# Attention scores with k's low part in two zero-padded tiles instead of one shared by the two halves of a head

## The chip, the cores and the metric

One core of a Trainium2 chip runs the whole program: TensorE (PE; its weight loads are shown apart as PEld), VectorE (DVE), ScalarE (ACT), GpSimd (POOL) and the queue SP, which issues DMAs. The metric is the device time of one execution in microseconds. The kernel before takes 956.73 us, the median of three runs (956.12 to 957.03).

## The reference

Two layers of a decoder trunk over 512 tokens of width 1024, in float32. Layer 0 projects the normalised tokens once and feeds two branches, differential attention and an mLSTM; layer 1 is a gated MLP with spatial mixing. The change lies in the attention of layer 0: 8 heads, each with two score maps of 64 channels, and a causal softmax for each.

```python
s = jnp.einsum('bhcqd,bhckd->bhcqk', qi, kt).astype(jnp.float32)   # c: the two halves of a head
s = jnp.where(k_pos[None, :] <= q_pos[:, None], s, -jnp.inf)
p = jax.nn.softmax(s, axis=-1)
a = p[:, :, 0] - lam * p[:, :, 1]
return jnp.einsum('bhqk,bhkv->bhqv', a.astype(vt.dtype), vt)
```

## The kernel before, in words

Every product of float32 operands is carried by float32r passes: an operand x is split into h (its upper 12 bits) and l = x - h, and h.h + h.l + l.h is accumulated in one PSUM bank. Weights come in as `raw` by DMA from SP's queue; ACT makes `wh` (L201), DVE or POOL `wl` (L203). A projection unit (`project`, `Unit.mm`, L251) multiplies all tokens by 512 columns: 8 k-tiles, 4 output banks `pj`, 3 products each.

All engines' orders are written out by hand: the program records instructions in the order of the Python code, and a counter of k-tiles (`clock`, `tick`) says after how many of them a step of the work beside the projections is recorded (`pump`). The attention of one half (4 heads, `attention(p)`, p = 0 or 1) runs so beside the projections that follow it: at each step one row block of 128 queries of one head gets its scores (`att_a`), an earlier one its softmax difference (`att_a2`), its transposes (`att_b`, L740) and its product with v (`att_c`, L752). Within a head the row blocks go 3, 2, 1, 0, so that scores have 512, 384, 256 and 256 columns.

q and k are laid for products over 128 partitions (rows of the array). A head's 128 channels are its two halves c of 64, in partitions LO (0 to 63) and HI (64 to 127). `qa` has, for c = 0, qh in LO and ql in HI; `ka` has kh in both, so that one product gives qh.kh + ql.kh (L716). `qb` and `kb` do the same for c = 1. What is missing, qh.kl, is a second product into the same bank (L718), over the 64 partitions of that half alone: `kl` holds kl of c = 0 in LO and of c = 1 in HI.

`da_k` makes these tiles from the projection's output: ACT rounds kh into one half (L682, L683), DVE subtracts for kl (L684, L685), POOL copies kh into the other half (L686, L687). Then `da_q` makes qa and qb (L695 to L699), then the attention begins. Scores take two PSUM banks (tag "s"), one for each c; DVE adds the causal mask (L720) and takes the maximum (L721), ACT the exponential with its sum (L722).

Large tiles live in named slots (`slot`), of which a later tile takes over what an earlier one has left: A0, A1, B0, B1, M0, M1, V0, V1, W0, W1, N0, H0 to H3.

Of the kernel before, what the change touches and what calls it, by code (L numbers as in the profile page):

```python
"""Two-layer hybrid decoder trunk (differential attention + mLSTM, then gMLP) on one core.

float32 products on the tensor engine are carried by three float32r passes: every operand
x is split exactly into h (12 significant bits) and l = x - h, and h.h + h.l + l.h is
accumulated in float32.
"""
# [4 lines left out]
F32 = _my.dt.float32  # L11
# [11 lines left out]
EPS = 1e-6  # L23
# [4 lines left out]
POOL0 = (2, 5, 7, 9, 11, 13, 15)  # L28
WB = 9        # split weight tiles on chip
ATT = ((4, 4, 4, 5), (5, 5, 6, 6))  # L30
# [16 lines left out]
SOFT2 = 0  # L47
AHEAD = 7     # how far their making runs ahead of their use

# columns of l0_w_in  # L50
DA_Q, DA_K, DA_V, DA_Z = 0, 1024, 2048, 3072
ML_QK, ML_V, ML_I, ML_O, ML_Z = 4096, 5120, 6144, 6152, 7176
# rows of the table of per-channel vectors
C_DAG, C_MLG, C_CW, C_CB, C_SG, C_N = 0, 1, 3, 35, 43, 59


def hybrid_kernel(tc, x, pre_g0, w_in0, b_ig, b_fg, conv_w, conv_b, lq1, lk1, lq2, lk2,
# [8 lines left out]
    with ExitStack() as ctx:  # L66
# [13 lines left out]

# [1 line left out]
        ident = wk.tile([P, P], F32, name="ident")  # L82
# [10 lines left out]
        def rstd_of(dst, ssum, n, k):  # L93
            """dst = (ssum / n + EPS) ** -0.5"""
            nc.vector.tensor_scalar(dst, ssum, 1.0 / n, EPS, ALU.mult, ALU.add)
            nc.gpsimd.tensor_tensor(dst, dst, mhalf[:, :k], ALU.pow)

# [1 line left out]
        rows = wk.tile([P, P], F32, name="rows", tag="sz", bufs=2)  # L99
# [30 lines left out]

        # the tensor engine's clock rises while it works
        warm = wk.tile([P, 512], BF16, name="warm", tag="aT", bufs=2)
# [27 lines left out]

# [1 line left out]
        # units of 512 columns in the order in which they are computed: weights, first column,  # L162
        # k-tiles in order
        up = lambda n: list(range(n))
# [48 lines left out]
        def later(dt, fn, soft=False):  # L213
            """emit fn after dt more k-tiles' products; a soft one not while it should be quiet"""
            clock["due"].append((clock["t"] + dt, fn, soft))
# [40 lines left out]
        def project(kind, ah, al, consumer, tail=2, quiet=None):  # L256
            """quiet: the function that the consumer needs, with no other work between the outputs"""
            un = Unit(kind, ah, al)
# [25 lines left out]

        # normalised tokens, transposed and split
        def norm_transpose(i, xns, hT, lT, hf, nm):
# [11 lines left out]

# [1 line left out]
        hT = [slot(f"H{k}", f"hT{k}", F32R) for k in range(2)]  # L300
# [35 lines left out]

# [1 line left out]
        def new_mv(p):  # L338
# [73 lines left out]

        # gates of the mLSTM: log-space weights per token (columns) and per chunk (rows)
        N0 = slot("N0", "n0misc", F32, (P, 2048))
# [20 lines left out]
        def gates():  # L435
# [15 lines left out]
            for c in range(4):  # L451
                nc.tensor.matmul(gps[:, c * 8:c * 8 + 8], lhsT=grow[:, c * P:(c + 1) * P],
                                 rhs=fold, start=True, stop=True)
            # gate columns: [token, (chunk, head)]
            gview = gps[:, 0:32].rearrange("p (c g) -> p c g", c=4)
            for dst, o in ((gi, 0), (xf, 4)):
# [3 lines left out]
                                        ALU.add)  # L460
            # log_sigmoid(x) = min(x, 0) - log1p(exp(-|x|)), log1p(e) = 2 artanh(e / (2 + e))
            ee = st(16, "ee")
# [15 lines left out]
            nc.vector.scalar_tensor_tensor(lf, xf, 0.0, acc, ALU.min, ALU.subtract)  # L478
            # lambda
            ldot = st(2, "ldot")  # L480
# [7 lines left out]
            yield  # L488
            # rows: [(chunk, head), position]
            rps = pst("s", "rps")  # L490
# [14 lines left out]
            nc.vector.tensor_copy(blR, cp2[:1, 0:32])  # L505
            mrow = wk.tile([1, 32], F32, name="mrow")       # m_prev of every chunk, M at its end
            nc.vector.memset(mrow, 0.0)
# [33 lines left out]
        def pump():  # L541
            """one step of the work beside the projections; a step says how long to wait after it"""
            while bg:
                try:
                    clock["next"] = clock["t"] + (next(bg[0]) or 4)
                    break
                except StopIteration:
                    bg.pop(0)
# [43 lines left out]

# [1 line left out]
        Cst = N0[:, 0:1032].rearrange("p (h d) -> p h d", h=4)  # L594
# [59 lines left out]

# [1 line left out]
        dq, dk, dv = {}, {}, {}  # L656
# [9 lines left out]
        def da_v(p):  # L666
            dv[p] = slot(f"V{p}", f"dv{p}")
            project("nat", ah0, al0, copy_consumer(dv[p]))

        # The heads' q and k split and stacked for K = 128: with c the half of a head that the  # L670
        # partitions hold, q[c] has qh in half c and ql in the other one, k[c] has kh in both,
        # and kl[c] is in half c.
        LO, HI = slice(0, 64), slice(64, 128)

        def da_k(p, tags):
            def f(i, o):
                if i == 0:
                    if p == 1:
                        drain(ga0)
                    dk[p] = [slot(t, f"{n}{p}", F32R) for t, n in zip(tags, ("ka", "kb", "kl"))]  # L680
                ka, kb, kl = dk[p]
                nc.scalar.copy(ka[LO, i, :], o[LO, :])  # L682
                nc.scalar.copy(kb[HI, i, :], o[HI, :])  # L683
                nc.vector.tensor_tensor(kl[LO, i, :], o[LO, :], ka[LO, i, :], ALU.subtract)  # L684
                nc.vector.tensor_tensor(kl[HI, i, :], o[HI, :], kb[HI, i, :], ALU.subtract)  # L685
                nc.gpsimd.tensor_copy(ka[HI, i, :], ka[LO, i, :])  # L686
                nc.gpsimd.tensor_copy(kb[LO, i, :], kb[HI, i, :])  # L687
            project("tr", ah0, al0, f)
# [14 lines left out]
        def att_a(p, h, i):  # L703
# [8 lines left out]
            for c in range(2):  # L712
                cc = (LO, HI)[c]
                s = pst("s", f"sc{nm}{c}")
                qs = dq[p][c][:, h, i * P:(i + 1) * P]
                nc.tensor.matmul(s[:, :n2], lhsT=qs, rhs=dk[p][c][:, h, 0:n2],  # L716
                                 start=True, stop=False)
                nc.tensor.matmul(s[:, :n2], lhsT=qs[cc, :], rhs=dk[p][2][cc, h, 0:n2],  # L718
                                 start=False, stop=True)
# [6 lines left out]
        def att_a2(pr, sm, nk, r0):  # L726
            """p0 - (lam s0 / s1) p1; the output takes the 1 / s0"""
            nc.vector.reciprocal(sm[:, 2:3], sm[:, 1:2])
            nc.vector.reciprocal(r0, sm[:, 0:1])
            nc.vector.scalar_tensor_tensor(sm[:, 3:4], sm[:, 2:3], nlam, sm[:, 0:1],  # L730
                                           ALU.mult, ALU.mult)
            nc.vector.scalar_tensor_tensor(pr[:, 0, :nk], pr[:, 1, :nk], sm[:, 3:4], pr[:, 0, :nk],
                                           ALU.mult, ALU.add)
# [22 lines left out]
        def head_norm(p, h):  # L756
            """the head's rmsnorm in four steps; a mean square beyond float32 gives rstd = 0, as an
            infinite one does"""
            o = ao.pop((p, h))
# [56 lines left out]

# [1 line left out]
        yh, yl = {}, {}  # L818
# [70 lines left out]
        da_v(0)  # L889
        da_k(0, ("A0", "A1", "B1"))  # L890
        drain(gm)
# [4 lines left out]
        ml_o(0)  # L896
        da_k(1, ("M0", "M1", "B1"))
        da_q(1, ("B0", "N0"))
# [3 lines left out]
        bg.append(da_z(0, ("A0", "A1")))  # L902
        bg.append(ml_z(0, ("M0", "M1")))
        bg.append(ml_z(1, ("V0", "W0")))
        drain(ga1)
        bg.append(da_z(1, ("B0", "B1")))

# [1 line left out]
        def out_project(layer, ah, al, post_g, h1, done, y0tag):  # L909
# [41 lines left out]
        def load_h1():  # L951
            for t, n in (("W1", "h1a"), ("V1", "h1b")):
                h1t.append(slot(t, n))
# [33 lines left out]

# [1 line left out]
        ah1 = lambda k: hT1[k // 4][:, k % 4, :]  # L989
# [3 lines left out]
        for j in range(4):  # L993
            vt = slot(("A0", "A1", "M0", "M1")[j], f"v1_{j}")
            v1.append(vt)
# [43 lines left out]
        for j in range(4):  # L1039
# [6 lines left out]
            project("tr", ah1, al1, fu)  # L1046
            tg = (("B0", "B1"), ("V0", "W0"), ("N0", "A0"), ("A1", "M0"))[j]
            y1h.append(slot(tg[0], f"y1h{j}", F32R))
# [57 lines left out]
```

## Time and profile before

| | us |
|---|---|
| median of three runs | 956.73 |
| span of the profiled execution, first to last instruction | 954.5 |
| TensorE busy in it | 939.4 |
| weight loads (beside the matmuls) | 753.3 |
| DVE busy | 458.5 |
| ACT busy | 410.4 |
| POOL busy | 179.1 |

The page gives the span of the profiled execution and no time of its own around it. Ends of matmuls are modelled, and matmuls overlap; their starts are what is to be read. "issue" behind an idle time is idle that no semaphore event explains. PEclk is the granted clock of TensorE as a share of 2.4 GHz. The attention of the first half lies between some 202 and 306 us, that of the second between 327 and 432.

### The profile page before, as it was taken

What the parts mean: (1) busy time and instruction counts of PE and PEld (TensorE: products, weight loads), DVE (VectorE), ACT (ScalarE), POOL (GpSimd) and SP (SyncE); (2) the same over time, 40 slices, a digit from 0 to 9 for tenths busy, and PEclk for the clock granted to TensorE, in tenths of its full rate; (3) what the DMA queues carried; (4) which work ended last, traced back from release to release, by engine and by line L of the source; (5) the groups of instructions that cost most, each with busy time, mean ns of one, the idle gap of its engine ahead of it and who ended that gap; (6) DMA issues with size and microseconds to landing.
All of it is one profiled execution on the core that took longest, in us unless ns stands there. A gap on an engine that the chain in (4) does not pass through costs nothing.

```text
span 954.5 us, 11642 instructions
## 1 busy us (share of the span) xinstructions
PE 939.4 (98%) x4259; PEld 753.3 (79%) x4259; DVE 458.5 (48%) x955; ACT 410.4 (43%) x876; POOL 179.1 (19%) x258
## 2 busy tenths in 40 slices
PE   7999999999999999999999999999999999999997
PEld 4778888877778777778888887888888888888885
DVE  4467555656656465664443355222634343434323
ACT  5334433445566445665443335444224242433311
POOL 3210022311245214444020022000010101011000
PEclk8999999999999999999999999999999999999998
DMA  8242222312112322222343313423223232314212
GB/s 270 69 132 90 89 67 63 93 45 67 54 58 89 89 66 67 62 72 71 105 155 133 111 45 110 133 91 109 90 69 107 67 111 67 110 67 133 89 45 88
DMA packets 45039, 86.94 MB, mean 91 GB/s; under 512 B 4715, under 2 KB 5046, under 8 KB 44854
## 3 DMA queue, kind: packets, MB, share of 16 engines
q1 hardware_dynamic: 43334, 80.29, 26.5%
q0 software_dynamic: 1504, 5.78, 1.7%
q8 instruction: 33, 0.54, 0.2%
q14 instruction: 24, 0.20, 0.1%
q10 hardware_dynamic: 144, 0.13, 0.0%
HBM read 84.08 MB, written 2.11 MB: 90 GB/s over the span
## 4 chain that ended last, share of the span: by engine, by line
PE 96%; DMA 1%; DVE 1%; issue 1%; SPq 0%; ACT 0%; POOLq 0%; POOL 0%; DVEq 0%; ACTq 0%
PE pj L251 83%; PE sc L718 2%; PE ao L752 2%; PE sc L716 2%; PE vs L1058 1%; PE at L740 1%; DMA raw<-in_l_w_in_dram 1%; PE yT L823 1%; PE mN L625 1%; PE xnT L289 1%; PE mN L627 1%; PE mU L631 1%; DVE xn_b L979 1%; PE gT L445 0%; PE mS L602 0%
## 5 line engine op out<-in xcount | busy, mean ns | idle before, releaser
L203 DVE TENSOR_TENSOR wl<-raw,wh 128x512 fp32r<-128x512 f32 x250 | 172.9, 712 | 254.3 <-ACT wh L201 253.8
L201 ACT CAST wh<-raw 128x512 fp32r<-128x512 f32 x287 | 169.4, 615 | 135.9 <-PE pj L251 120.8
L251 PE MATMUL pj<-wh,hT 128*128 128x512 f32 x448 | 183.1, 409 | 0.7 <-ACT hT L292 0.7
L251 PE MATMUL pj<-hT,wh 128*128 128x512 f32 x448 | 180.8, 403 | 0.0
L251 PE MATMUL pj<-hT,wl 128*128 128x512 f32 x448 | 177.1, 395 | 0.0
L251 PE MATMUL pj<-lT,wh 128*128 128x512 f32 x448 | 177.1, 395 | 0.0
L251 PE MATMUL pj<-wh,lT 128*128 128x512 f32 x448 | 176.9, 395 | 0.0
L251 PE MATMUL pj<-wl,hT 128*128 128x512 f32 x448 | 176.6, 394 | 0.0
L251 PEld LDWEIGHTS pj<-wh,hT 128*128 128x128 f32 x448 | 85.0, 190 | 22.8 <-issue 3.4
L251 PEld LDWEIGHTS pj<-wh,lT 128*128 128x128 f32 x448 | 84.8, 189 | 19.6 <-DVE lT L293 0.6
L251 PEld LDWEIGHTS pj<-hT,wl 128*128 128x128 f32 x448 | 84.2, 188 | 20.4
L251 PEld LDWEIGHTS pj<-hT,wh 128*128 128x128 f32 x448 | 84.3, 188 | 19.6 <-issue 0.5
L251 PEld LDWEIGHTS pj<-lT,wh 128*128 128x128 f32 x448 | 84.3, 188 | 18.6
L251 PEld LDWEIGHTS pj<-wl,hT 128*128 128x128 f32 x448 | 85.1, 190 | 16.0
L203 POOL TENSOR_TENSOR wl<-raw,wh 128x512 fp32r<-128x512 f32 x38 | 52.1, 1373 | 135.5 <-ACT wh L201 131.8
L251 PE MATMUL pj<-wh,yh 128*128 128x512 f32 x128 | 51.4, 402 | 0.0
L722 ACT ACTIVATE p<-sc,nm 128x512 f32<-128x512 f32 (+3 forms) x64 | 33.7, 527 | 39.8 <-DVE nm L721 36.8
L251 PE MATMUL pj<-wh,yl 128*128 128x512 f32 x128 | 50.5, 395 | 0.0
L251 PE MATMUL pj<-wh,y1h 128*128 128x512 f32 x128 | 50.3, 393 | 0.0
L251 PE MATMUL pj<-wl,yh 128*128 128x512 f32 x128 | 50.3, 393 | 0.0
L251 PE MATMUL pj<-wh,y1l 128*128 128x512 f32 x128 | 50.3, 393 | 0.0
L1054 POOL TENSOR_TENSOR sz<-gu,sz 128x512 f32<-128x512 f32 x16 | 21.1, 1317 | 155.5 <-ACT sz L1053 155.5
(255 smaller groups left out, 1147.0 us busy)
## 6 DMA issues: line engine op xcount, KB each, us to landing
raw<-in_l_w_in_dram SPq DMA_DIRECT2D x112, 512.0 KB, 3.7
raw<-in_l_w_out_dram SPq DMA_DIRECT2D x32, 512.0 KB, 3.3
x<-in_x_dram SPq DMA_DIRECT2D x3, 512.0 KB, 9.9
nMb<-scr POOLq DMA_DIRECT2D x1, 1024.0 KB, 4.8
pg<-in_l_post_g_dram POOLq DMA_DIRECT2D x2, 512.0 KB, 4.3
h1a<-in_x_dram POOLq DMA_DIRECT2D x2, 512.0 KB, 4.2
h1b<-in_x_dram POOLq DMA_DIRECT2D x2, 512.0 KB, 4.9
out_dram<-h1a SPq DMA_DIRECT2D x4, 256.0 KB, 2.0
```

Source lines behind the costliest of these rows:

```text
L201: nc.scalar.copy(wh, raw[:, n % 2, :])
L203: eng.tensor_tensor(wl, raw[:, n % 2, :], wh, ALU.subtract)
L251: nc.tensor.matmul(self.outs[i], lhsT=a, rhs=b, start=(n == 0 and m == 0), stop=(n == len(self.ks) - 1 and m == ms[-1]))
L289: nc.tensor.transpose(b[:, k * P:(k + 1) * P], xns[:, hf, k * P:(k + 1) * P], ident)
L625: nc.tensor.matmul(o[:, 0:258], lhsT=mt[:, 0, :], rhs=va, start=True, stop=(c == 0))
L627: nc.tensor.matmul(o[:, 0:258], lhsT=mt[:, 3, :], rhs=Cst[:, h, :], start=False, stop=True)
L631: nc.tensor.matmul(u[:, 0:258], lhsT=mt[:, 4, :], rhs=va, start=True, stop=True)
L716: nc.tensor.matmul(s[:, :n2], lhsT=qs, rhs=dk[p][c][:, h, 0:n2], start=True, stop=False)
L718: nc.tensor.matmul(s[:, :n2], lhsT=qs[cc, :], rhs=dk[p][2][cc, h, 0:n2], start=False, stop=True)
L722: nc.scalar.activation(pr[:, c, :nk], s[:, :nk], AF.Exp, bias=nmx[:, c:c + 1], accum_out=sm[:, c:c + 1])
L752: nc.tensor.matmul(o[:, i * P:(i + 1) * P], lhsT=aT[:, kb * P:(kb + 1) * P], rhs=dv[p][:, kb, h * P:(h + 1) * P], start=(kb == 0), stop=(k ...
L1054: nc.gpsimd.tensor_tensor(sz, gus[i // 2][:, i % 2, :], sz, ALU.mult)
```

## The change

The tile `kl` becomes two, `kla` and `klb`. Each holds kl of its half of the heads in that half's 64 partitions, and zeros in the other 64, which POOL writes once for each p. The second score product then runs over all 128 partitions, with the same `qs` as the first; the other part of q meets the zeros. The second tile needs a slot more, so several tiles change places: the second v goes to M0, the k tiles of p = 1 to M1, A0, B1 and V1, and later tiles that stood in M0 stand in V1 (and the other way round).

```diff
-            dv[p] = slot(f"V{p}", f"dv{p}")
+            dv[p] = slot(("V0", "M0")[p], f"dv{p}")
...
-                    dk[p] = [slot(t, f"{n}{p}", F32R) for t, n in zip(tags, ("ka", "kb", "kl"))]
-                ka, kb, kl = dk[p]
+                    dk[p] = [slot(t, f"{n}{p}", F32R) for t, n in zip(tags, ("ka", "kb", "kla", "klb"))]
+                    for t, half in zip(dk[p][2:], (HI, LO)):
+                        nc.gpsimd.memset(t[half, :, :].bitcast(F32), 0.0)
+                ka, kb, kla, klb = dk[p]
...
-                nc.vector.tensor_tensor(kl[LO, i, :], o[LO, :], ka[LO, i, :], ALU.subtract)
-                nc.vector.tensor_tensor(kl[HI, i, :], o[HI, :], kb[HI, i, :], ALU.subtract)
+                nc.vector.tensor_tensor(kla[LO, i, :], o[LO, :], ka[LO, i, :], ALU.subtract)
+                nc.vector.tensor_tensor(klb[HI, i, :], o[HI, :], kb[HI, i, :], ALU.subtract)
...
-                cc = (LO, HI)[c]
...
-                nc.tensor.matmul(s[:, :n2], lhsT=qs[cc, :], rhs=dk[p][2][cc, h, 0:n2],
+                nc.tensor.matmul(s[:, :n2], lhsT=qs, rhs=dk[p][2 + c][:, h, 0:n2],
                                  start=False, stop=True)
...
-        da_k(0, ("A0", "A1", "B1"))
+        da_k(0, ("A0", "A1", "B1", "V1"))
...
-        da_k(1, ("M0", "M1", "B1"))
+        da_k(1, ("M1", "A0", "B1", "V1"))
...
-        bg.append(ml_z(0, ("M0", "M1")))
+        bg.append(ml_z(0, ("V1", "M1")))
...
-            for t, n in (("W1", "h1a"), ("V1", "h1b")):
+            for t, n in (("W1", "h1a"), ("M0", "h1b")):
...
-            vt = slot(("A0", "A1", "M0", "M1")[j], f"v1_{j}")
+            vt = slot(("A0", "A1", "V1", "M1")[j], f"v1_{j}")
...
-            tg = (("B0", "B1"), ("V0", "W0"), ("N0", "A0"), ("A1", "M0"))[j]
+            tg = (("B0", "B1"), ("V0", "W0"), ("N0", "A0"), ("A1", "V1"))[j]
```

POOL's queue before, where the k of the first half is made: the last step of the mLSTM on POOL (L612), the copies of kh into the other half, then weight splits of the unit after the next. In brackets stands what a row waits for.

```order
L612 TENSOR_TENSOR mt_1539<-mt_1539,mq 128x128 [waits Activation_49]
L686 COPY ka_1578<-ka_1578 64x512 [waits DMAHW3_49,Activation_49,Pool_49]
L687 COPY kb_1579<-kb_1579 64x512 [waits Activation_49]
L686 COPY ka_1578<-ka_1578 64x512 [waits Activation_49]
L687 COPY kb_1579<-kb_1579 64x512 [waits Activation_49]
```

The same place in the changed kernel, whose lines are numbered one or two higher:

```order
L612 TENSOR_TENSOR mt_1539<-mt_1539,mq 128x128 [waits Activation_49]
L682 MEMSET kla_1580 64x2048 [waits Pool_49]
L682 MEMSET klb_1581 64x2048
L688 COPY ka_1578<-ka_1578 64x512 [waits DMAHW3_49,Activation_49]
L689 COPY kb_1579<-kb_1579 64x512 [waits Activation_49]
L688 COPY ka_1578<-ka_1578 64x512 [waits Activation_49]
L689 COPY kb_1579<-kb_1579 64x512 [waits Activation_49]
```

Two memsets stand ahead of the copies; the same two stand at the same place of the second half. The queues of DVE, ACT and SP hold the same instructions in the same order, with the same waits.

TensorE's queue before, at the first score group of the first half, between two projection products:

```order
L251 MATMUL pj_0_1794<-wh_0_1683,lT_119 128x512
L716 MATMUL sc_1805<-ka_1578,qa_1635 128x512 [waits Activation_49,Pool_49]
L718 MATMUL sc_1805<-kl_1580,qa_1635 128x512
L716 MATMUL sc_1811<-kb_1579,qb_1636 128x512 [waits Activation_49,Pool_49]
L718 MATMUL sc_1811<-kl_1580,qb_1636 128x512
L251 MATMUL pj_0_1794<-wh_1_1699,hT_117 128x512
```

And in the changed kernel:

```order
L251 MATMUL pj_0_1797<-wh_0_1686,lT_119 128x512
L717 MATMUL sc_1808<-ka_1578,qa_1638 128x512 [waits Activation_49,Pool_49]
L719 MATMUL sc_1808<-kla_1580,qa_1638 128x512
L717 MATMUL sc_1814<-kb_1579,qb_1639 128x512 [waits Activation_49,Pool_49]
L719 MATMUL sc_1814<-klb_1581,qb_1639 128x512
L251 MATMUL pj_0_1797<-wh_1_1702,hT_117 128x512
```

No product is moved, added or taken away, and the waits are the same; the second product of each pair reads another tile (the sizes printed are those of the output).

## Rows read from the trace of the kernel before

**Rows 1.** The page, part 1: busy us (share of span) xinstructions.

```profile
PE 939.4 (98%) x4259; PEld 753.3 (79%) x4259; DVE 458.5 (48%) x955; ACT 410.4 (43%) x876; POOL 179.1 (19%) x258
```

**Rows 2.** Waits of TensorE: us in total, times, longest; first and last of four.

```profile
PE xnT L289 <- DVE xn_a L330: 3.8, 3, 3.0
...
PE pj L251 <- ACT hT L292: 0.7, 1, 0.7
```

**Rows 3.** The chain that ended last: start us, us, what; a stretch of projections alone.

```profile
65.43 48.07 PE pj L251 x207
```

**Rows 4.** Timeline: start us, us, engine, line, out<-in, size [idle before]; first score group.

```profile
202.65 0.39 PE L716 MATMUL sc<-ka,qa 128*128 128x512 f32 x1
...
202.97 0.49 PE L718 MATMUL sc<-kl,qa 64*128 64x512 f32 x1
...
203.39 0.49 PE L716 MATMUL sc<-kb,qb 128*128 128x512 f32 x1
203.81 0.18 PEld L718 LDWEIGHTS sc<-kl,qb 64*128 64x128 f32 x1 [0.24 <-issue]
203.81 0.50 PE L718 MATMUL sc<-kl,qb 64*128 64x512 f32 x1
...
204.24 0.51 PE L251 MATMUL pj<-wh,hT 128*128 128x512 f32 x1
...
204.58 0.40 PE L251 MATMUL pj<-wl,hT 128*128 128x512 f32 x1
```

**Rows 5.** Timeline: second products of the groups of 384 and of 256 columns.

```profile
208.45 0.44 PE L716 MATMUL sc<-kb,qb 128*128 128x384 f32 x1
...
208.82 0.44 PE L718 MATMUL sc<-kl,qb 64*128 64x384 f32 x1
...
213.03 0.38 PE L716 MATMUL sc<-kb,qb 128*128 128x256 f32 x1
...
213.34 0.38 PE L718 MATMUL sc<-kl,qb 64*128 64x256 f32 x1
```

**Rows 6.** Timeline: eight 16-row products of the gates (L452) and the projection behind them.

```profile
47.37 0.96 PEld L452 LDWEIGHTS gps<-fold,n0misc 16*128 16x128 f32 x8 [0.37 <-issue]
...
48.35 0.50 PE L251 MATMUL pj<-hT,wh 128*128 128x512 f32 x1
...
48.70 0.40 PE L251 MATMUL pj<-lT,wh 128*128 128x512 f32 x1
```

**Rows 7.** Timeline: eight products of 128 columns with v, and what comes next.

```profile
216.51 1.05 PE L752 MATMUL ao<-dv,aT 128*128 128x128 f32 x8
...
217.40 0.49 PE L740 MATMUL at<-ident,p 128*128 128x128 f32 x3
```

**Rows 8.** POOL: a memset, copies grouped (busy, mean ns), last copy; TensorE: the score behind.

```profile
1.31 0.20 POOL L85 MEMSET tri<- 128x128 f32 x1
...
L686 POOL CAST ka<-ka 64x512 fp32r<-64x512 f32 x8 | 6.0, 746 | 2.9 <-issue 1.9 <-ACT ka L682 0.5
...
308.90 0.96 POOL L687 CAST kb<-kb 64x512 fp32r<-64x512 f32 x1
...
327.76 0.39 PE L716 MATMUL sc<-ka,qa 128*128 128x512 f32 x1
```

**Rows 9.** Timeline: ends of two exponentials' sums, and DVE's product of p.

```profile
207.87 0.19 ACT L722 ACTIVATION_READ_ACCUMULATOR p<-sc,nm 128x1 f32 x1
...
209.66 0.75 DVE L732 SCALAR_TENSOR_TENSOR p<-p,sm 128x512 f32<-128x512 f32 x1
...
212.52 0.19 ACT L722 ACTIVATION_READ_ACCUMULATOR p<-sc,nm 128x1 f32 x1
```

**Rows 10.** All waits: DVE for the scores of TensorE, us in total, times, longest.

```profile
DVE sc L720 <- PE sc L718: 23.1, 19, 3.1
```

**Rows 11.** Windows: us, busy (x) of PE, PEld, DVE, ACT, POOL, granted clock, DMA.

```profile
10.00:20.00 10.00, 8.95 (x35) 6.22 (x36) 7.85 (x12) 5.55 (x11) 3.10 (x4) 0.78 1.02 356
...
202.00:306.00 104.00, 104.00 (x479) 80.11 (x478) 64.68 (x172) 58.20 (x158) 33.75 (x62) 1.00 0.20 61
```

## The prediction

> **What bounds the kernel now.** I read the first part of the page first: TensorE is busy 939.4 of the 954.5 us of the span, the next engine 458.5 [rows 1]. Then the waits of TensorE by releaser: there are four rows, 8.2 us in all, and the last of them is worth 0.7 us; none of the four is in the attention, they lie in the two norms, the warm-up and the first products [rows 2]. So between 202 and 432 us, where the two attention halves run between the projections' products, the end is set by how fast TensorE gets through its own queue. The view to read there is the order in time with its start times: matmuls overlap, and the distance from one start to the next is what a product costs, not its duration.
>
> A projection product (512 columns, 128 rows) costs 48.07 us / 207 = 0.232 us [rows 3]. In the first score group the same size costs more: from the 64-row product to the next 128-row one 0.42 us, from there to the next 64-row one 0.42, from there to the projection 0.43, and the second projection product still comes 0.34 after the first; the very first 64-row product comes 0.32 after the score product ahead of it [rows 4]. The weight load of a 64-row product shows 0.24 us of idle ahead of it that no event explains ("issue") [rows 4]: loads elsewhere are done under the matmul before, this one waits for it.
>
> **What the change removes.** From the first score product's start to the second projection product's start the group of 512 columns takes 204.58 - 202.65 = 1.93 us [rows 4]; five products at 0.232 are 1.16. So 0.77 us per group is lost, four times 0.19: once at each of its four boundaries between 128 and 64 rows. For the smaller shapes a boundary costs 208.82 - 208.45 = 0.37 at 384 columns and 213.34 - 213.03 = 0.31 at 256 [rows 5]; in proportion to columns a product there is worth 0.174 and 0.116, which leaves 0.196 and 0.194. The loss is the same at every size, so it belongs to the boundary and not to the columns. A second place in the program bears this out: eight 16-row products at 47.37 us have the same unexplained idle of 0.37 us ahead of their first weight load, all eight loads then run through in 0.96 us (0.12 apart at most), and the second 128-row product behind them comes 0.35 after the first [rows 6]. Few rows alone cost nothing there; going in and out does.
>
> The changed kernel has 32 score groups (2 halves, 4 heads, 4 row blocks) of four 128-row products, so all 128 boundaries go: 32 x 0.77 = 24.6 us off TensorE's queue.
>
> The bounds of that: a 256-column product has to cost 0.116 for it, and no 256-column float32r product at 128 rows on both sides stands in the trace. The nearest rows from below are the eight products of [rows 7], 217.40 - 216.51 = 0.89 us for eight, 0.111 each with a weight load for each. From above, the duration of one weight load is 0.19 us [rows 4]; if loads could not overlap each other, 256 and 384 columns would cost 0.19 and the saving falls by 16 x 4 x 0.074 + 8 x 4 x 0.016 = 5.2 us, to 19.4. I take the lower one, since loads in [rows 7] do overlap.
>
> **A rule that speaks against it.** The two 64-row products of a group start 203.81 - 202.97 = 0.84 us apart, with a full-height product between them [rows 4]; nothing of them overlaps. The Trainium skill, "TensorE: Matmul & The Clock Gate", Part 3, says that products with few rows, laid at different row groups, run at the same time, and its closing table advises slicing small contractions that way. By that rule padding throws away a chance of hiding one of the two, some 32 x 0.16 = 5 us; but that chance was not taken by the kernel before, so by the trace nothing of it is lost here.
>
> **What the change adds.** Four memsets on POOL of 64 x 2048, two ahead of each half's copies of k. The nearest rows: a memset of 128 elements per partition takes 0.20 us, a copy of 512 per partition 0.746 [rows 8]. The first scaled by 16 gives 3.2 us, the second by 4 gives 3.0; a fixed part inside these would make it less, down to some 1.6. So POOL's copies end 3 to 6.5 us later per half. Behind them in POOL's queue stand the weight splits of later units, and the score products wait for the copies. The copies end at 309.86 and the first score product that needs them starts at 327.76 [rows 8]: 17.9 us of cover, with the projection of q in between; the first half is alike. Cost nothing. Cover is gone only if one memset took over 8 us. The two subtractions on DVE stay, into two tiles instead of one. The swaps of slots (the second v into the former query slot of the mLSTM, kb of the second half into the slot of ka of the first) add no wait to any engine's row, and what the slots held is drained before. No DMA is added, and SP's queue keeps its order.
>
> **What becomes late next.** A group that TensorE reaches earlier must still find its PSUM bank free: a score bank is released by the exponential of the step before. In the first steps DVE and ACT are no faster: DVE's long product of p, which hangs on the exponentials alone, is at work from 209.66 to 210.41 [rows 9], when the second group is already computed, and only then comes DVE's next work on scores; so their times stay put. The second group's second half started at 208.45 [rows 5], and the bank's last reader ended at 207.87 + 0.19 = 208.06 [rows 9]: 0.39 us of room. TensorE would come 0.77 + 0.39 (two boundaries of its own group) = 1.16 earlier, so it waits 0.77. In the third group the room is 213.03 - (212.52 + 0.19) = 0.32 [rows 5, 9], the lead 1.16 again, the wait 0.84. Together 1.6 us. Later DVE itself waits for scores, 23.1 us over 19 of its 64 times [rows 10], so there the elementwise chain has slack to follow. I allow 1.0 us for further short waits, an estimate between 0 and 3.
>
> **The sum.** 24.6 - 1.6 - 1.0 = 22.0 us off a span of 954.5: 932.5. The page gives the span alone; the median of the timed runs, 956.7, is 2.2 above it, and I carry these 2.2 over: **934.7 us**.
>
> **The rivals.**
> - *Weight loads set the pace.* At 256 and 384 columns a product costs 0.19, the upper bound above. 19.4 saved, less 1.5 of waits: 17.9, 938.8 us. For it: no such product stands in the trace. Against: 0.111 apart in [rows 7].
> - *The elementwise chain takes over.* In 45 of 64 steps DVE does not wait for scores, and in the first steps the chain is the slower side. If that held all along, only the steps in which DVE waits would gain: 19/64 of 24.6 is 7.3, some 949 us. Against: the 23.1 us of [rows 10] are spread over both halves, and the busy shares of DVE and ACT there are 0.62 and 0.56 [rows 11].
> - *The boundary is not the cause.* If the idle came from adding a second product to a bank, or from reading q twice, the padded products would keep it, and the time would be 956.7. Against: the projections add 24 products to one bank at 0.232, the projection behind a group pays too, and so do the 16-row products of [rows 6].
> - *Slower, by the clock.* The granted clock is 1.00 (2.4 GHz) in the attention and fell to 0.78 in the 10 us of the start around and behind a wait of TensorE of 3.0 us at once [rows 2, 11]. If the new waits in the first groups brought the lower level, 1.2 GHz, it would cost half of each stretch at it; the change comes out slower once more than 44 us of the attention are run at the lower level (22 us lost), for instance 960 with 50. Against: the waits worked out are under 0.9 us each, three times shorter than that one.
>
> **How the numbers follow.** The forecast (931 to 937, that is 20 to 25 saved) gets 0.66, weight loads 0.17, the elementwise chain 0.08, no effect 0.05, slower 0.02; 0.02 is left for a larger gain, below 930. Forecast and weight loads hold 0.83; their ends, with the bounds of the waits (0 to 3 us) and of the load, are 930.5 and 941.5. That is the range. The measurement tells 0.2%, 1.9 us, from no change. Faster: 0.66 + 0.17 + 0.08 + 0.02 = 0.93; same 0.05; slower 0.02.
>
> **What would show it.** Right: in the changed kernel's order in time the four score products of 512, 384 and 256 columns start about 0.23, 0.17 and 0.12 apart, the projection product behind them follows at once, and no weight load of a score product has unexplained idle ahead of it; the stretch from the first score product to the last is about 22 us shorter, and the waits of TensorE gain a row "sc <- ACT p" of one to two us, in the second and third group. Starts 0.19 apart at 256 columns show the rival of weight loads; idle ahead of the second product of each pair, still there, shows that the boundary was not it; a row of score products that wait for POOL would show that the memsets are not covered; many rows of waits for DVE or ACT between 202 and 432 us show the elementwise chain. A granted clock under 0.95 in the attention would show the fourth.

## The result, and the profile after

The changed kernel takes 935.43 us (median of four runs, 934.87 to 935.66) against 956.42 for the kernel before beside it: a ratio of 0.9783, 95% interval 0.9769 to 0.9797, so 21.0 us or 2.2% less. The span of its profiled execution is 933.5 us.

Part 1 of its page, to be set against [rows 1]:

```profile
PE 916.7 (98%) x4259; PEld 749.0 (80%) x4259; DVE 458.0 (49%) x955; ACT 408.6 (44%) x876; POOL 185.7 (20%) x262
```

TensorE has the same 4259 matmuls and is busy 22.7 us less. DVE and ACT do the same work; POOL does 6.6 us more. The first score group in the order in time (columns as in [rows 4]):

```profile
203.37 0.39 PE L717 MATMUL sc<-ka,qa 128*128 128x512 f32 x1
203.60 0.39 PE L719 MATMUL sc<-kla,qa 128*128 128x512 f32 x1
203.83 0.40 PE L717 MATMUL sc<-kb,qb 128*128 128x512 f32 x1
204.06 0.39 PE L719 MATMUL sc<-klb,qb 128*128 128x512 f32 x1
204.29 0.39 PE L251 MATMUL pj<-wh,hT 128*128 128x512 f32 x1
204.52 0.39 PE L251 MATMUL pj<-wl,hT 128*128 128x512 f32 x1
```

All starts are 0.23 apart, and from the first to the sixth it is 1.15 us, where [rows 4] had 1.93. The fourth group, of 256 columns:

```profile
217.92 0.28 PE L719 MATMUL sc<-kla,qa 128*128 128x256 f32 x1
218.04 0.28 PE L717 MATMUL sc<-kb,qb 128*128 128x256 f32 x1
218.16 0.28 PE L719 MATMUL sc<-klb,qb 128*128 128x256 f32 x1
218.28 0.39 PE L251 MATMUL pj<-wh,hT 128*128 128x512 f32 x1
```

0.12 apart, where [rows 5] had 0.31. A group of 384 columns, behind the first of its products:

```profile
227.00 0.34 PE L719 MATMUL sc<-kla,qa 128*128 128x384 f32 x1
227.18 0.34 PE L717 MATMUL sc<-kb,qb 128*128 128x384 f32 x1
227.36 0.34 PE L719 MATMUL sc<-klb,qb 128*128 128x384 f32 x1
```

0.18 apart. (In groups that stand behind transposes, in both kernels, the first product's start is shown 0.03 us behind the last transpose, where transposes are 0.11 apart, and the next product 0.08 later than its columns ask for. The sum is the same; such groups are read from the second product on.) By the starts in the two traces, the stretch from the first score product to the last went from 225.2 to 204.4 us, 20.8 less. What lies before it and behind it differs by less than 1 us each, and by as much between the two traces of the changed kernel; so small differences are read below from the stretch of the scores.

What TensorE waits for in the attention, new against [rows 2]; three rows of its waits (us in total, times, longest), and one of its weight loads:

```profile
PE pj L251 <- ACT mz L869: 1.2, 1, 1.2
...
PE sc L717 <- ACT p L723: 0.6, 2, 0.3
PE pj L251 <- ACT mo L852: 0.2, 1, 0.2
...
PEld sc L717 <- ACT p L723: 2.1, 5, 0.6
```

The second group, in the timeline:

```profile
207.51 0.39 PE L251 MATMUL pj<-wh,lT 128*128 128x512 f32 x1
207.91 0.44 PE L717 MATMUL sc<-ka,qa 128*128 128x384 f32 x1
208.19 0.34 PE L719 MATMUL sc<-kla,qa 128*128 128x384 f32 x1
208.84 0.44 PE L717 MATMUL sc<-kb,qb 128*128 128x384 f32 x1 [0.31 <-ACT p L723]
209.12 0.34 PE L719 MATMUL sc<-klb,qb 128*128 128x384 f32 x1
209.30 0.40 PE L251 MATMUL pj<-wh,hT 128*128 128x512 f32 x1
```

From 207.51 to 209.30 it is 1.79 us; 0.23 and four times 0.174 are 0.93. So the wait costs 0.86 us: 0.17 ahead of the first score product, 0.48 ahead of the third, and 0.10 behind each of these two. The row of waits names only 0.31 of it: a matmul counts as busy until its modelled end, and part of the wait lies under that; and the loads of the two products that wait start with them, at 207.91 and 208.84, each followed by the next load only 0.11 later, so that the product behind comes late too. The third group loses as much:

```profile
212.06 0.60 PE L741 MATMUL at<-ident,p 128*128 128x128 f32 x4
212.69 0.39 PE L717 MATMUL sc<-ka,qa 128*128 128x256 f32 x1
...
213.49 0.38 PE L717 MATMUL sc<-kb,qb 128*128 128x256 f32 x1 [0.30 <-ACT p L723]
...
213.84 0.39 PE L251 MATMUL pj<-wh,hT 128*128 128x512 f32 x1
```

1.78 us against 4 x 0.11 + 4 x 0.117 = 0.91: 0.87. The largest is at the end of a projection in the second half, where a projection bank is still being read by ACT:

```profile
403.74 0.40 PE L251 MATMUL pj<-wh,lT 128*128 128x512 f32 x1
405.36 0.50 PE L251 MATMUL pj<-wh,hT 128*128 128x512 f32 x1 [1.23 <-ACT mz L869]
405.70 0.39 PE L251 MATMUL pj<-wl,hT 128*128 128x512 f32 x1
```

1.96 us for two products, 1.5 too many. With some 0.4 at the other bank (mo) and 0.3 in the second and third group of the second half the waits of the attention come to 3.9 us. Together with the 20.8 that were gained this is 24.7, which is what the boundaries were worked out to cost.

On the other side, DVE's wait for scores, which was 23.1 us in [rows 10]:

```profile
DVE sc L721 <- PE sc L719: 5.2, 7, 2.3
```

DVE used to wait for TensorE; now it does so for less than a quarter of that time.

### The profile page after: what moved, and what is told of

It is laid out like the page before. It is cut to its first block, busy times and chain, and to the rows that moved or that the text cites. A ratio compares the mean times of both kernels' runs of the same rounds, so it can differ in the third digit from the quotient of the medians.

```text
span 933.5 us, 11645 instructions
## 1 busy us (share of the span) xinstructions
PE 916.7 (98%) x4259; PEld 749.0 (80%) x4259; DVE 458.0 (49%) x955; ACT 408.6 (44%) x876; POOL 185.7 (20%) x262
## 4 chain that ended last, share of the span: by engine, by line
PE 89%; DVE 4%; ACT 4%; issue 1%; DMA 1%; POOL 1%; SPq 0%; POOLq 0%; DVEq 0%; ACTq 0%
PE pj L251 79%; PE vs L1059 2%; PE ao L753 2%; DVE nm L722 1%; ACT wh L201 1%; ACT p L723 1%; DMA x<-in_x_dram 1%; PE sc L717 1%; PE yT L824 1%; PE mN L625 1%; PE sc L719 1%; PE at L741 1%; PE xnT L289 1%; PE mU L631 1%; PE mN L627 1%
## 5 line engine op out<-in xcount | busy, mean ns | idle before, releaser
L251 PE MATMUL pj<-wh,hT 128*128 128x512 f32 x448 | 179.8, 401 | 2.0 <-ACT mz L869 1.2
L251 PE MATMUL pj<-wl,y1h 128*128 128x512 f32 x128 | 50.3, 393 | 0.0
```

The costliest lines, as they stand in the source:

```text
L251: nc.tensor.matmul(self.outs[i], lhsT=a, rhs=b, start=(n == 0 and m == 0), stop=(n == len(self.ks) - 1 and m == ms[-1]))
```

## The experiments

Each is measured against runs of the kernel before on the same chip (956.1 to 956.8 us). Times are medians.

| run | us | what is in it |
|---|---|---|
| before | 956.4 | four boundaries between 128 and 64 rows per score group |
| changed | 935.43, again 935.46 | none |
| e1_rows64 | 956.05 | the changed kernel, second products over 64 rows |
| e2_one_padded | 944.91 | two boundaries, one 64-row product |
| e3_adjacent64 | 942.01 | two boundaries, two 64-row products side by side |
| e4_memsets3 | 936.03 | three times the memsets |
| e5_no_second | 933.29 | no second products |
| e10_no_mask | 930.33 | changed, without DVE's mask |
| e9_no_second_no_mask | 924.02 | neither |
| e6, e7 (first steps) | 937.09, 937.70 | early score groups later |
| e11_shifted | 936.29 | the same, later steps kept in place |
| e12_two_on_pool | 934.63 | two weight splits from DVE to POOL |

### Was it the boundary?

**e1_rows64**: the number of rows undone, all else as changed.

```diff
-                nc.tensor.matmul(s[:, :n2], lhsT=qs, rhs=dk[p][2 + c][:, h, 0:n2],
+                cc = (LO, HI)[c]
+                nc.tensor.matmul(s[:, :n2], lhsT=qs[cc, :], rhs=dk[p][2 + c][cc, h, 0:n2],
                                  start=False, stop=True)
```

> The changed kernel with one part undone: the second score product runs over the 64 partitions of its half again, reading kla or klb there. The two tiles, their slots, the four memsets and the order of all queues stay as changed. Theory (each change between 128 and 64 rows in TensorE's queue costs about 0.19 us, 128 of them): the whole gain goes, 956.4 us give or take 1, with the starts 0.42, 0.37 and 0.31 apart as before, and the memsets and slots cost nothing. Rival (part of the gain comes from the new places of the tiles or from POOL's memsets): between 936 and 952.

956.05 us, ratio to the kernel before 0.9997 (0.9988 to 1.0007). The whole gain hangs on the rows; the slots, the second tile and the memsets cost and give nothing that can be measured.

**e2_one_padded**: only c = 0 padded.

```diff
-                nc.tensor.matmul(s[:, :n2], lhsT=qs, rhs=dk[p][2 + c][:, h, 0:n2],
+                cc = (slice(0, P), HI)[c]
+                nc.tensor.matmul(s[:, :n2], lhsT=qs[cc, :], rhs=dk[p][2 + c][cc, h, 0:n2],
                                  start=False, stop=True)
```

> As the changed kernel, but only c = 0 has the zero-padded second product; for c = 1 it runs over 64 partitions. Two boundaries between 128 and 64 rows per group instead of none, 64 in all. Theory: 64 x 0.19 = 12.3 us of the 24.6 come back, and the early waits of TensorE are shorter by about 1 us than in the changed kernel: 945 us (944 to 947). Theory that the 64-row product itself costs 0.39 more, wherever it stands: the same 945. Rival (elementwise chain sets the pace beyond the first gain): nearer 937.

944.91 us. The first group in its timeline, from its third product on:

```profile
203.91 0.40 PE L717 MATMUL sc<-kb,qb 128*128 128x512 f32 x1
204.23 0.50 PE L720 MATMUL sc<-klb,qb 64*128 64x512 f32 x1
204.66 0.50 PE L251 MATMUL pj<-wh,hT 128*128 128x512 f32 x1
205.00 0.39 PE L251 MATMUL pj<-wl,hT 128*128 128x512 f32 x1
```

0.32, 0.43 and 0.34 where 0.23 each would do: 0.40 us for two boundaries. Half the boundaries, half the loss. That does not yet tell a boundary from a product that is dear wherever it stands; the next run does.

**e3_adjacent64**: both second products over 64 rows again, but next to each other.

```diff
-            for c in range(2):
-                s = pst("s", f"sc{nm}{c}")
...
+            for c, full, first in ((0, True, True), (0, False, False), (1, False, True), (1, True, False)):
+                cc = slice(0, P) if full else (LO, HI)[c]
+                k = dk[p][c if full else 2 + c]
+                nc.tensor.matmul(ss[c][:, :n2], lhsT=qs[c][cc, :], rhs=k[cc, h, 0:n2],
+                                 start=first, stop=not first)
```

> As e1 (both second products over 64 partitions), but the four products of a group stand in the order 128 rows (c = 0), 64 rows (c = 0, partitions 0 to 63), 64 rows (c = 1, partitions 64 to 127), 128 rows (c = 1). Two boundaries per group, two 64-row products next to each other. Boundary theory: 945 us (944 to 947), and the second 64-row product starts 0.23 (512 columns) behind the first. If the change from one half of the rows to the other costs as much as one from 128 to 64: three boundaries, 950.5. Theory that each 64-row product costs 0.39: 956.4. Rule of the Trainium skill, TensorE: Matmul & The Clock Gate, Part 3 (products at different row groups run at the same time): the second starts a few ns behind the first and some 5 us more are saved, 940.

942.01 us. Its first group:

```profile
202.68 0.39 PE L719 MATMUL sc<-ka,qa 128*128 128x512 f32 x1
203.00 0.49 PE L719 MATMUL sc<-kla,qa 64*128 64x512 f32 x1
203.01 0.49 PE L719 MATMUL sc<-klb,qb 64*128 64x512 f32 x1
203.43 0.50 PE L719 MATMUL sc<-kb,qb 128*128 128x512 f32 x1
203.76 0.40 PE L251 MATMUL pj<-wh,hT 128*128 128x512 f32 x1
204.00 0.40 PE L251 MATMUL pj<-wl,hT 128*128 128x512 f32 x1
```

The two 64-row products start together and share one slot of 0.42 us (by the starts they are 0.01 us apart or less in all groups that do not wait for a bank). From the first score product to the second projection product it is 1.32 us: 1.93 before, 1.15 with padding. A 64-row product is therefore not dear in itself: here the second costs nothing. Going in and out costs 0.39, and overlapping saves one product: 0.23, 0.17 or 0.12. So a single pair is better padded at all three sizes, and by little at 512. The time lies 2 us above what the rule of overlap would have given (940), and 3 below the boundary theory alone; the stretch of the scores is 4.0 us shorter than in e2 (209.8 against 213.8), where 5 were expected. By the steps some 0.7 of the missing 1 us lies in the second and the fourteenth, where TensorE waits for a bank; in the second and third group it is the second of the two 64-row products that waits, so these pairs do not overlap.

**e4_memsets3**: POOL's cover.

```diff
-                    for t, half in zip(dk[p][2:], (HI, LO)):
+                    for t, half in 3 * tuple(zip(dk[p][2:], (HI, LO))):
```

> The changed kernel with each memset written three times, so four more of 1.8 us ahead of each half's copies on POOL, 7.2 us per half. Theory (POOL's copies have room: in the changed kernel the copies of the second half end at 304.62 and the first score product that needs them starts at 318.12, 13.5 us): the same time, 935.4 give or take 0.7. Rival (the copies are on TensorE's path): up to 2 x 7.2 us longer, 950.

936.03 us (934.79 to 936.79): no more than the scatter, and the stretch of the scores is the same 204.4 us. The last memset and the last copy of the second half, and (TensorE) the first score product that needs them:

```profile
303.94 1.80 POOL L682 MEMSET klb<- 64x2048 f32 x1
...
310.86 0.61 POOL L689 CAST kb<-kb 64x512 fp32r<-64x512 f32 x1
...
318.53 0.39 PE L717 MATMUL sc<-ka,qa 128*128 128x512 f32 x1
```

With 7.2 us more on POOL there are still 7 us of room.

### What comes next?

**e5_no_second**: the second products left out.

```diff
                 nc.tensor.matmul(s[:, :n2], lhsT=qs, rhs=dk[p][c][:, h, 0:n2],
-                                 start=True, stop=False)
-                nc.tensor.matmul(s[:, :n2], lhsT=qs, rhs=dk[p][2 + c][:, h, 0:n2],
-                                 start=False, stop=True)
+                                 start=True, stop=True)
```

> The changed kernel without any second score product (the term qh.kl is left out), 64 products fewer, no boundary added. Price of the padded products by their spacing in the changed kernel: 2 x (8 x 0.231 + 8 x 0.176 + 16 x 0.117) = 10.3 us. Theory (TensorE's queue is the bound, the elementwise chain follows but for short waits): 10.3 less some 2.5 us of more waits in the second and third group and at the two places where a projection bank is late: 927.7 us (926 to 930). Rival (after the first gain DVE and ACT set the pace): under 4 us saved, 932 to 935.

933.29 us: 2.1 us saved, not 7.7. The theory that TensorE's queue goes on being the bound fell here, and the time lies in the range of its rival. Four rows of what TensorE waits for, and DVE's wait for scores:

```profile
PE sc L717 <- ACT p L721: 2.9, 8, 0.5
PE pj L251 <- ACT mz L867: 2.0, 1, 2.0
...
PE pj L251 <- ACT dz L829: 1.1, 1, 1.1
PE pj L251 <- ACT mo L850: 1.0, 1, 1.0
```

```profile
DVE sc L719 <- PE sc L717: 2.8, 3, 2.0
```

By the starts, steps without a wait are 0.2 to 0.5 us shorter, as 64 fewer products would have it; others are up to 1.4 longer, and the two halves together gain 1.9 us. By these rows the room that DVE and ACT had, 23.1 us of waiting in [rows 10], was nearly used up by the change itself.

**e9_no_second_no_mask** and **e10_no_mask** test that by making the chain of DVE and ACT shorter.

```diff
-                nc.vector.tensor_tensor(s[:, i * P:nk], s[:, i * P:nk], tri, ALU.add)
```

> The kernel without second score products (it took 933.3 us) and also without DVE's addition of the causal mask to the scores, so neither qh.kl nor the mask is in the output: 64 additions of 0.29 us less on DVE, 18.6 us. If the chain of DVE and ACT is what kept that kernel from its 10.3 us, the chain is shorter now by about 0.6 us per step and TensorE gets most of them: 926 to 928. Rival (it was something else, a projection bank or a weight that is late whatever DVE does): 932 to 934.

> The changed kernel without DVE's addition of the causal mask alone (the mask is missing from the output). If the chain costs the changed kernel only the waits that its trace shows, 1.7 us in the second and third group and 1.4 at two projection banks, at most these go: 933 give or take 1. If the chain holds the changed kernel back more than that: under 931.

Without the mask's addition the changed kernel takes 930.33 us and the one without second products 924.02. Between these two the second products are worth 6.3 us (7.3 by the stretch of the scores, 200.9 and 193.6), with the mask 2.1. So it was the chain that held e5 back, for the larger part: the price of 10.3 is not reached here either. 924.02 is also less than the 926 to 928 that were expected. In e10 the first half's steps (first score group to sixteenth) take 68.95 us instead of 70.54, the second's 87.31 instead of 89.18: 3.5 us of the 3.9 that were read off the changed kernel as waits. 1.5 and 0.4 of it come back at the two projection banks, 1.2 of 1.7 in the first three steps, 0.3 in the second half. The other 1.6 us of its 5.1 lie outside the attention, where the two traces of the changed kernel differ by over 1 us ahead of it and as much behind it. By the time alone, under 931, e10 would speak for a chain that costs more than its waits; by the trace it does not. DVE waits for scores again in e10:

```profile
DVE nm L721 <- PE sc L719: 14.4, 11, 2.8
```

**e6_first_steps5, e7_first_steps6, e11_shifted**: the early waits, taken by recording the second and third score group of the first half later.

```diff
-                yield ATT[p][items[n][1]] if n < len(items) else 4
+                yield (5 if p == 0 and n < 2 else ATT[p][items[n][1]]) if n < len(items) else 4
```

> The changed kernel with 5 instead of 4 k-tiles of projection between the first, second and third score group of the first half. Theory (the waits of the second and third group for the exponentials, 0.86 and 0.87 us by the starts, are made by the two groups coming too early, and a k-tile is 0.70 us of work): 0.7 us of each is filled, 934.0 against 935.4. Rival (the wait only moves to the fourth group or to the next projection): 935.4.

> The same with 6 k-tiles. Theory: both waits are filled in full, 1.7 us, 933.7 against 935.4. Rival (moved, not filled): 935.4.

> The changed kernel as it is, on the same chip and beside the two before it, as their measure: 935.4 us, give or take 0.7.

> The changed kernel with one k-tile more ahead of the second and of the third score group of the first half, and one less behind its eighth and twelfth, so that later steps stand where they stood. Theory: the early waits are filled, some 1.2 us, 934.2 against 935.4 to 935.5. Rival (the chain needs the time, wherever the wait is taken): 935.4 or a little more, with new waits near the eighth and twelfth group.

(The first step had 5 k-tiles already, so that e6 adds one and e7 three; e11 adds one at each of the two steps and takes one away at each of two later ones.) 937.09, 937.70 and 936.29 us, against 935.46 for the changed kernel beside e6 and e7: all three forecasts failed. e11 came out as its rival had it, e6 and e7 slower than even their rivals (935.4). The stretch of the scores is 206.5, 205.2 and 205.4 us, against 204.4; of the 2.2 us that e7 loses only 0.8 lies in it, and where the rest comes from is not known. At the place itself the waits did fill in part: the first three steps take 14.35 us in the changed kernel and the same in e6 with one more k-tile of 0.70 in them, 14.96 in e7 with three more. (In e6 the wait of the second group stays as it was, since the step ahead of it is no longer than before; that of the third falls to 0.2, and the fourth group gets one of 0.3.) It was lost further on: in e6 the thirteenth and fourteenth step take 14.6 us together instead of 12.3 (13.2 in e7), and in both the next unit waits at its banks:

```profile
PE pj L251 <- DVE klb L687: 1.2, 1, 1.2
```

The attention is held while a projection's last products are made (`quiet`), and a step that comes one k-tile late falls into that stretch; that this is the mechanism is read from the code and was not tried by itself. In e11 the steps that were cut to three k-tiles run without a wait (3.42 us), but the fourteenth takes 8.37 instead of 7.40 and the wait for mo is 1.1 instead of 0.2: the wait moved.

**e12_two_on_pool**: instead of the timetable, the chain.

```diff
         on_pool.update((18, n) for n in PU18)
+        on_pool.update(((7, 6), (7, 7)))
```

> The changed kernel with two of DVE's weight splits (the seventh and eighth of the unit that runs when the first half's attention begins) given to POOL; the result is the same. In the changed kernel DVE takes such a split at 209.33, after 1.35 us of waiting for ACT's cast, between the exponentials of the first group and its softmax difference. Theory: without it the second group's maxima come 1.1 us sooner, and the wait of the third group, 0.87 us, goes; that of the second (0.86), which hangs on the first group's exponentials, stays: the three first steps take 13.5 instead of 14.35 us, and the kernel 934.6 against 935.4 and 935.5. Rival (another wait takes its place): 14.35 and 935.4.

934.63 us (933.03 to 935.35), and by the trace the first three steps take 13.54 us instead of 14.35; all later ones are the same to 0.01. The wait of the third group is gone, that of the second stays. The whole, 0.8 us, is what the trace gives; the timed runs of the two kernels touch, so by them alone it is not told apart. Its median is the lowest of the versions in which no product and no mask is left out.

## Why the prediction held, point by point

- **The bound.** That TensorE's own queue set the end in the attention was right for the kernel before: e1 and e2 move by the boundaries, but for the short waits. It is no longer so behind the change (e5).
- **The price of a boundary**, 0.19 us, and the sum of 24.6 us: right (20.8 gained and 3.9 of waits). It does not fall once at each boundary, though: by the starts the five distances of a group lose 0.09, 0.19, 0.19, 0.20 and 0.11. Starts after are 0.23, 0.18 and 0.12 apart, as forecast, and e2 with half the boundaries lies 11.8 us below the kernel before beside it and 9.5 above the changed one. (The last two boundaries give less than the first two, since by then the waits take a share.)
- **256 columns at 0.116**: measured 0.118 (0.114 to 0.122 where nothing waits). The rows chosen for it were misread in part: the eight rows of [rows 7] are four products in plain float32 (`att_c` makes 80, the trace has 160 records), each recorded twice, so 0.111 is the distance from one load and pass to the next and not the cost of a product; that loads can follow so closely is what the choice needed. The rival of weight loads at 0.19 fell; a load still takes 0.19 there, but under the products before it.
- **The memsets.** 1.81 us each (a group's row of the changed kernel: count | busy us, mean ns | idle before), near the lower end of 1.6 to 3.2:

```profile
L682 POOL MEMSET kla<- 64x2048 f32 x2 | 3.6, 1807 | 0.1
```

  They are free, as e4 shows with three times as many.
- **The waits at the start**: 1.6 us forecast for the second and third group, 0.77 and 0.84; measured 0.86 and 0.87. The difference is about the 0.10 by which the product behind a wait comes late. The sign, a row "sc <- ACT p" of one to two us, came as 0.6 us on TensorE's row and 2.1 on that of its weight loads. The mechanism, a score bank still read by the exponential of the step before, is what the trace names, and e12 takes one of the two away by its cause.
- **The further waits**: this term was too small, 1.0 allowed and 2.2 found, 1.5 of it at one projection bank (mz). The prediction looked at score banks alone; that its allowance, which named no place, came within 1.2 us is luck. So 21.0 us were saved instead of 22.0. That the time is only 0.7 above 934.7 comes from the kernel before, which took 956.42 beside the changed one and not the 956.73 that the forecast set out from.
- **The range** (930.5 to 941.5) does not come out of its terms: 24.6 saved without any wait gives 932.1, and 19.4 saved with waits of 1.6 and 3 gives 941.9.
- **The rule against it.** The prediction wrote that nothing is lost by padding since the two products do not overlap in the kernel before. True of that kernel; but the rule of the Trainium skill, TensorE: Matmul & The Clock Gate, Part 3, holds here once they stand side by side (e3: starts 0.01 us apart or less). What padding gives up is about 4 us of overlap; the two boundaries per group that it saves outweigh them, and it comes out 6.6 us ahead of e3.
- **The elementwise chain** got 0.08 as a rival. It did not decide this change, yet it was next in line: e5, which takes work of another 10.3 us off TensorE, gained 2.1. The steps in which DVE waits for scores were the measure of its room, and 23.1 us of room stood against 24.6 us of gain. That comparison stood in the prediction's rows and was not made.
- **The clock** stayed at 1.00 (2.4 GHz) in the attention, at waits of at most 1.2 us by their rows; a window of each half in the changed kernel (columns as in [rows 11]):

```profile
202.60:300.00 97.40, 96.56 (x496) 80.87 (x495) 67.59 (x177) 61.14 (x168) 37.19 (x64) 1.00 0.25 71
...
320.00:412.00 92.00, 90.78 (x472) 77.09 (x471) 62.43 (x162) 59.03 (x156) 36.30 (x52) 1.00 0.25 74
```

## What to carry to other kernels

Count the changes of the number of rows in TensorE's queue, not the products with few rows: read start to start, subtract what the columns cost, and a constant remainder at each change is its price. Where few-row products come one at a time between full ones, pad them with zeros; where several can stand together on different halves of the rows, set them side by side, and compare one product saved per pair with two boundaries per visit. And before adding up what a faster engine gains, set it against the time that its partners now wait for it. Here that time was an upper bound and no more: 20.8 us were gained of 23.1, with 5.2 left e5 gained 1.9 of 10.3, and with 14.4 (e10) the same products were worth 7.3.

## What was not expected of the hardware

Two float32r products over partitions 0 to 63 and 64 to 127, into different banks, started 0.01 us apart or less and together took what one takes (0.42 us at 512 columns, a boundary included). And the time that TensorE lost to a wait was larger than the trace's row of waits tells: 0.86 us by the starts, 0.31 by the row.
